# A block of RG-LRU, retention and gated MLP on one core: norm factors spread through DRAM, first loads on two queues, last scalings shared with GpSimd, one more buffer

## The chip, the cores and the metric

The kernel runs on one NeuronCore of a Trainium2 chip. The metric is the device time of one execution in microseconds, taken as the median over several runs. Profiles come from the hardware profiler, one execution each. In them PE is TensorE (PEld its weight loads), DVE VectorE, ACT ScalarE, POOL GpSimd and SP the sync engine, on whose queue nearly all transfers are issued.

## What is computed

One decoder block on x of shape (1, 2048, 1024) in float32. Cut to what matters:

```
u = rms_norm(x, norm1_gain);  proj = u @ w_in                  # 1024 -> 3072
x_lru, g_lru, q, k, v, g_ret = split(proj)
hl = rg_lru(causal_conv(x_lru))                                # a scan over the sequence
y_lru = rms_norm(hl * gelu(g_lru), lru_norm_gain)
o = head_group_norm(retention_chunkwise(rotary(q), rotary(k), v))
y_ret = o * silu(g_ret)
h = x + concat(y_lru, y_ret) @ w_out                           # 1024 -> 1024
u = rms_norm(h, norm2_gain)
a, b = split(causal_conv(u @ ffn_up_w))                        # 1024 -> 2 * 3072
h = h + (gelu(a) * b) @ ffn_down_w                             # 3072 -> 1024
out = rms_norm(h, final_norm_gain)
rms_norm(x, g) = x / sqrt(mean(x * x) + eps) * g               # one factor for each position
```

## The kernel before

Channels lie on the 128 partitions, positions on the free axis. The 2048 positions are two groups (g = 0, 1) of 1024, which the program calls HT. The stages follow one another on TensorE: A (input projection with the LRU and retention work) of g 0, A of g 1, B (output projection) of both, U (up projection, convolution, gate) of both, D (down projection in three parts c = 0, 1, 2) of both. A `Unit` multiplies two weight tiles of 128x1024 by the stage's input as seven block products of a Winograd scheme (p1 to p7, 12 matmuls each); a `PlainUnit` does eight ordinary quarter products of 12 matmuls. Each float32 operand is split into a high and a low part, both in the float32r form (`split`, `split_here`: ACT makes the high part, DVE the low one), and three matmuls stand for one product.

Work is held in SLOTS buffers of 128x1024 and eight PSUM banks. No instruction order is written out: generator processes ask for buffers, banks and operations, and `Flow` (lines 190 to 316) plays them against a cost for each operation (`Engine.cost_*`, `Op.kb` for a transfer) and gives each engine a fixed order, by readiness and a priority in ticks (one tick is one product). LEAD is how many ticks ahead weights may be asked for, RAW how many ticks ahead the split of an input block gets its priority. Every engine then runs its list in order, SP and ACT their transfers too.

A norm needs one factor for each position, and the positions lie along the free axis. `rstd` (line 985) sums the squares over partitions with one matmul for each 128 positions (tile `mst`), which puts the sums on partitions as [128, 8] (tile `ms`), scales them on DVE and raises them to -0.5 on POOL. `spread` (line 970) then makes the [128, 1024] tile `rb`, the same in every partition: eight matmuls of the broadcast factor column against the identity (tile `pb`, two groups of four), and two ACT copies from PSUM. It is called by `norm1` for both groups (line 1030), by the LRU norm of both groups (line 1123), by stage B's norm of both groups and stage D's of group 0 (`NormGroup`, line 1352), and for the last output three times on parts of 512, 256 and 256 positions (`FinalGroup.piece`, line 1400). DVE then multiplies the data by gain and `rb`.

At the start the raw x blocks of the first units are scaled by a gain column of the vector tile `vec` (`RawStage.bring`, line 548), and the first weight tile comes in two halves (`PlainUnit.first`, line 728).

Of the kernel before, what the change touches and what calls it, by code (L numbers as in the profile page):

```python
# [25 lines left out]
F32 = mybir.dt.float32  # L26
# [14 lines left out]
SLOTS = 54  # L41
# [3 lines left out]
BACKLOG = 10.0  # L45
RATE = 330.0
# [12 lines left out]
RAW = 3  # L59
LEAD = 10  # L60
# [42 lines left out]
class Engine:  # L103
# [55 lines left out]
    def cost_p(self, op, n, args, kw):  # L159
        return 1.0 if op != "dma_start" else 0.1  # L160
# [159 lines left out]
def hymba_block_kernel(ctx: ExitStack, tc: tile.TileContext, xh, xn, win, wout, wup, down, gates, vecs,  # L320
# [96 lines left out]
    vec = cp.tile([P, V_N], F32, name="vec")  # L417
    idt = cp.tile([P, P], F32, name="idt")
    sml = cp.tile([P, 2, NH], F32, name="sml")
    ones = cp.tile([P, P], F32, name="ones")  # L420
# [13 lines left out]
    def setup():  # L434
        yield v.memset(ones, 1.0)
        z = yield Slot("z")
        yield v.memset(z[:, 0:Q], 0.0)
        y = yield Bank("sm", "y0")
        for i in range(WARM):
            yield pe.matmul(y, ones, z[:, 0:Q], start=True, stop=True)  # L440
        free(z, y)
# [99 lines left out]
    class RawStage(Stage):  # L541
# [6 lines left out]
        def bring(self, name, i, need, start):  # L548
            k, n = int(name[0]) - 1, int(name[1]) - 1
            yield Until(start)  # L550
            r = yield (Slot("raw", F32R) if self.gain is None else Slot("raw"))
            if self.gain is None:
                yield from self.src[2 * k + i].get_half(r.bitcast(F32), n)
            else:
                for m in range(2):
                    yield dma(r[:, half(m)], self.src[2 * i + m].t[:, k, half(n)])
            yield need - 2
            if self.gain is None:
                self.blk[name, i] = yield from split_here(r, "b")
            else:  # L560
                hi = yield Slot("bh", F32R)
                lo = yield Slot("bl", F32R)
                for m in range(2):
                    yield a.activation(hi[:, half(m)], r[:, half(m)], AF.Copy, scale=col(self.gain + 4 * i + 2 * m + k))
                    yield v.scalar_tensor_tensor(out=lo[:, half(m)], in0=r[:, half(m)], scalar=col(self.gain + 4 * i + 2 * m + k),
                                                 in1=hi[:, half(m)].bitcast(F32), op0=ALU.mult, op1=ALU.subtract)
                self.blk[name, i] = (hi, lo)
                free(r)
            self.event(name, i).on = True
# [124 lines left out]
    class PlainUnit:  # L694
# [20 lines left out]
        def weights(self, t0):  # L715
# [21 lines left out]
            def part(i, need, k, r, hi, lo):  # L737
                yield dma(r[:, half(k)], self.wsrc[i][:, half(k)])
# [230 lines left out]

    def spread(rt, c0, c1, r):  # L970

        yield have["idt"]
        for b in range(c0, c1, Q):
# [7 lines left out]
            yield op  # L981
            yield a.copy(r[:, b - c0:b - c0 + w], pb[:, 0:w])
            free(pb)

    def rstd(acc, n, r, c0=0, c1=HT):

        nb = (c1 - c0) // P
        rt = sp.tile([P, NCH], F32, tag="ms", name="ms")[:, 0:nb]
        pm = yield Bank("sm", "mst")
        op = None  # L990
        for t in range(nb):
            o = pe.matmul(pm[:, t:t + 1], acc[:, c0 + t * P:c0 + (t + 1) * P], ones[:, 0:1], start=True, stop=True)
            op = op + o if op else o
# [4 lines left out]
        yield from spread(rt, c0, c1, r)  # L998
# [31 lines left out]
    def norm1(g, start, due):  # L1030

        ms = sp.tile([P, NCH], F32, tag="ms1", name="ms1")
        left = [NCH]

        def one(t):
# [6 lines left out]
            if left[0] == 0:  # L1042
# [3 lines left out]
                yield from spread(ms, 0, HT, r)  # L1046
# [346 lines left out]
    class FinalGroup(NormGroup):  # L1393
# [6 lines left out]
        def piece(self, m, t, c0, c1):  # L1400
# [127 lines left out]
    def vectors():  # L1528
        yield dma(vec, vecs)
# [111 lines left out]
```

## Time and profile before

| | us |
|---|---|
| median of 3 runs | 2193.12 (2189.13 to 2193.19) |
| the profiled execution's own time | 2191.24 |
| its span in the profile | 2189.1 |
| PE busy | 2159.5 |
| DVE, ACT, POOL busy | 1767.8, 1244.6, 44.4 |

The span is the time from the first to the last recorded instruction, 2.1 us less than the execution's own time. Busy times overlap between engines. A profile line names an operation by the tile that it writes and the tiles that it reads (`pb<-idt,ms`); a float32 matmul that is not float32r leaves two records.

### The profile page before, as it was taken

The numbers are of one execution on the slowest core, as the hardware profiler recorded it, in microseconds if no ns is written. First come the engines' busy times: TensorE is split into PE (matmuls) and PEld (weight loads), VectorE is DVE, ScalarE is ACT, GpSimd is POOL, SyncE is SP. The second block draws the span as 40 slices with busy tenths as digits, with TensorE's granted clock in tenths as the row PEclk, the third lists the DMA queues.
The fourth block names the chain that finished last, engine by engine and source line by source line (L and its number), as shares of the span: only waits on it lengthen the run. The fifth ranks groups of instructions, "written<-read, shape, count | busy, mean of one in ns | idle before, by whom it ended". The sixth has DMA issues, their size and how long they took to land.

```text
span 2189.1 us, 26790 instructions
## 1 busy us (share of the span) xinstructions
PE 2159.5 (99%) x9938; PEld 1781.6 (81%) x9938; DVE 1767.8 (81%) x2228; ACT 1244.6 (57%) x1795; POOL 44.4 (2%) x30
## 2 busy tenths in 40 slices
PE   9999999999999999999999999999999999999998
PEld 6878878888788888888888888888888788887887
DVE  6999888877773688889788997888878987788875
ACT  6774775566632166666666766666666544444441
POOL 0010000000000000000000000000000000000000
PEclk9999999999999999999999999999999999999999
DMA  8965464133674954444333532322335787589762
GB/s 324 368 211 194 134 215 157 61 117 98 205 258 149 381 193 145 163 158 150 102 97 139 212 113 90 116 94 101 113 121 180 267 308 261 219 295 348 267 252 77
DMA packets 140530, 407.83 MB, mean 186 GB/s; under 512 B 15728, under 2 KB 20208, under 8 KB 140400
## 3 DMA queue, kind: packets, MB, share of 16 engines
q1 hardware_dynamic: 139248, 405.08, 52.5%
q8 instruction: 78, 1.28, 0.2%
q10 hardware_dynamic: 1152, 1.05, 0.1%
q14 instruction: 52, 0.43, 0.1%
HBM read 272.63 MB, written 125.04 MB: 182 GB/s over the span
## 4 chain that ended last, share of the span: by engine, by line
PE 94%; DVE 2%; DMA 1%; ACT 1%; issue 1%; SPq 0%; POOL 0%; POOLq 0%; DVEq 0%
PE py L124 33%; PE px L124 22%; PE pe L124 22%; PE pq L124 12%; PE po L124 1%; PE pa L124 1%; PE pb L124 1%; PE sc L124 1%; PE pt L124 1%; PE pk L124 1%; DVE raw L124 0%; PE mst L124 0%; DVE res L124 0%; DMA h<-res 0%; DMA h<-h 0%
## 5 line engine op out<-in xcount | busy, mean ns | idle before, releaser
L124 DVE TENSOR_TENSOR wl<-s,wh 128x1024 fp32r<-128x1024 f32 x182 | 222.3, 1221 | 90.9 <-ACT wh L124 83.5
L124 PE MATMUL py<-bh,wh 128*128 128x512 f32 x728 | 285.8, 393 | 3.4 <-DVE res L124 2.4
L124 PE MATMUL px<-raw,wh 128*128 128x512 f32 x728 | 284.1, 390 | 4.8 <-DVE raw L124 4.8
L124 PE MATMUL px<-bh,wh 128*128 128x512 f32 x728 | 285.8, 393 | 0.1
L124 PE MATMUL pe<-bh,wl 128*128 128x512 f32 x728 | 283.5, 389 | 2.3 <-DVE wl L124 2.3
L124 ACT CAST wh<-s 128x1024 fp32r<-128x1024 f32 x182 | 190.8, 1048 | 166.6 <-DVE s L124 150.3
L124 PE MATMUL pe<-raw,wh 128*128 128x512 f32 x728 | 283.4, 389 | 1.5 <-DVE raw L124 1.5
L124 PE MATMUL pe<-bh,wh 128*128 128x512 f32 x728 | 284.6, 391 | 0.0
L124 PE MATMUL py<-bh,wl 128*128 128x512 f32 x728 | 284.1, 390 | 0.0
L124 PE MATMUL px<-bh,wl 128*128 128x512 f32 x728 | 284.0, 390 | 0.0
L124 PE MATMUL py<-raw,wh 128*128 128x512 f32 x728 | 283.8, 390 | 0.0
L124 DVE SCALAR_TENSOR_TENSOR c<-o,vec,c 128x1022 f32<-128x1022 f32 x192 | 244.4, 1279 | 6.2
L124 PE MATMUL py<-bh,wv 128*128 128x512 f32 x728 | 240.4, 391 | 2.2 <-ACT o L124 1.4
L124 ACT COPY o<-py 128x512 f32<-128x512 f32 x204 | 119.5, 586 | 188.7 <-PE py L124 188.0
L124 DVE TENSOR_TENSOR raw<-raw,bh 128x1024 fp32r<-128x1024 f32 x158 | 188.8, 1218 | 3.3 <-ACT bh L124 3.3
L124 ACT CAST bh<-raw 128x1024 fp32r<-128x1024 f32 x158 | 161.3, 1050 | 36.7 <-DMA raw<-g_T 12.4
L124 PE MATMUL pq<-bh,wh 128*128 128x512 f32 (+1 forms) x432 | 168.2, 389 | 1.1 <-ACT bh L124 1.1
L124 PE MATMUL pq<-bh,wl 128*128 128x512 f32 (+1 forms) x432 | 165.7, 383 | 0.0
L124 PEld LDWEIGHTS py<-bh,wh 128*128 128x128 f32 x728 | 137.1, 188 | 33.9 <-DVE res L124 2.9
L124 PEld LDWEIGHTS px<-bh,wh 128*128 128x128 f32 x728 | 136.8, 188 | 33.6 <-issue 2.8
L124 PEld LDWEIGHTS px<-raw,wh 128*128 128x128 f32 x728 | 137.0, 188 | 33.3 <-DVE raw L124 5.7
L124 PEld LDWEIGHTS py<-bh,wv 128*128 128x128 f32 x728 | 136.7, 188 | 33.3 <-ACT o L124 1.6
(137 smaller groups left out, 3848.5 us busy)
## 6 DMA issues: line engine op xcount, KB each, us to landing
wa<-in_dram SPq DMA_DIRECT2D x91, 512.0 KB, 3.8
wb<-in_dram SPq DMA_DIRECT2D x91, 512.0 KB, 4.7
h<-res SPq DMA_DIRECT2D x56, 512.0 KB, 3.6
g_T<-t SPq DMA_DIRECT2D x96, 256.0 KB, 2.3
raw<-g_T SPq DMA_DIRECT2D x48, 512.0 KB, 7.2
res<-h SPq DMA_DIRECT2D x48, 512.0 KB, 6.9
g<-c SPq DMA_DIRECT2D x76, 256.0 KB, 3.0
raw<-g SPq DMA_DIRECT2D x38, 512.0 KB, 8.1
```

The costliest lines, as they stand in the source:

```text
L124: return Op(self.name, lambda: fn(*args, **kw), us, writes, reads, func=func)
```

## The change

Six of the ten spreads (`norm1` of group 1, the LRU norm of both groups, stage B's of both and stage D's of group 0) go through DRAM: `spread_far` stores the factors from [128, 8] into a DRAM row of 1024 and reads the row back into all partitions with two broadcast transfers, all three on SP's queue. `norm1` of group 0 keeps the matmuls and the copies. The three spreads of the last output keep the matmuls, but DVE reads the PSUM tile `pb` directly. Of the last two parts (256 positions each) two of the eight tiles are scaled by their gain on ACT beforehand and by the factor on POOL, from an ACT copy of `pb`.

At the start the gains of the first norm get a tile of their own, loaded first on ACT's queue together with one half of the first weight tile; the big vector tile is loaded later, and the first high part is made on DVE. `ones` shrinks to one column, some small tiles have fewer buffers and the scratch for dynamic transfers is smaller; SLOTS goes from 54 to 55, LEAD from 10 to 12, RAW from 3 to 4. So `Flow` plans every engine's order anew.

```diff
-SLOTS = 54
+SLOTS = 55
+SMALL = 600
-RAW = 3
-LEAD = 10
+RAW = 4
+LEAD = 12
...
     def cost_p(self, op, n, args, kw):
-        return 1.0 if op != "dma_start" else 0.1
+        return 0.1 if op == "dma_start" else max(1.0, 0.3 + 2.2e-3 * n)
...
+    gain1 = cp.tile([P, KT], F32, name="gain1")
-    ones = cp.tile([P, P], F32, name="ones")
+    ones = cp.tile([P, 1], F32, name="ones")
...
-            yield pe.matmul(y, ones, z[:, 0:Q], start=True, stop=True)
+            yield pe.matmul(y, z[:, 0:P], z[:, 0:Q], start=True, stop=True)
...
             else:
+                if name == "11" and i == 0:
+                    yield -20
                 for m in range(2):
                     yield dma(r[:, half(m)], self.src[2 * i + m].t[:, k, half(n)])
...
-                    yield a.activation(hi[:, half(m)], r[:, half(m)], AF.Copy, scale=col(self.gain + 4 * i + 2 * m + k))
+                    gain = gain1[:, 4 * i + 2 * m + k:4 * i + 2 * m + k + 1]
+                    if name == "11" and i == m == 0:
+                        yield v.tensor_scalar(out=hi[:, half(m)], in0=r[:, half(m)], scalar1=gain, scalar2=None, op0=ALU.mult)
+                    else:
+                        yield a.activation(hi[:, half(m)], r[:, half(m)], AF.Copy, scale=gain)
...
-                yield dma(r[:, half(k)], self.wsrc[i][:, half(k)])
+                yield dma(r[:, half(k)], self.wsrc[i][:, half(k)], "sp" if k else "a")
...
+    def spread_far(rt, r):
+        row = dp.tile([NCH, P], F32, name="row", tag=f"row{len(rows)}")
+        rows.append(row)
+        there = row.rearrange("t p -> p t")
+        yield Op("sp", lambda: nc.sync.dma_start(there, rt), ISSUE, parts(row), parts(rt), kb=SMALL)
+        n = HT // 2
+        for h in range(2):
+            src = row[h * 4:h * 4 + 4].rearrange("(o t) p -> o (t p)", o=1).to_broadcast([P, n])
+            yield dma(r[:, half(h)], src)
...
             yield op
+            if r is None:
+                return pb
             yield a.copy(r[:, b - c0:b - c0 + w], pb[:, 0:w])
...
-        yield from spread(rt, c0, c1, r)
+        if r is None:
+            return (yield from spread(rt, c0, c1, r))
+        yield from spread_far(rt, r)
...
-                yield from spread(ms, 0, HT, r)
+                yield from spread_far(ms, r) if g else spread(ms, 0, HT, r)
...
-                r = yield Slot("rb")
-                r = r[:, 0:c1 - c0]
-                yield from rstd(self.ss.acc, D, r, c0, c1)
+                n_p = 2 if c0 else 0
+                ys = [t[:, c0:c1] for _, t in sorted(self.t.items())]
+                for k in range(n_p):
+                    yield a.activation(ys[k], ys[k], AF.Copy, scale=col(V_NF + k))
+                pb = yield from rstd(self.ss.acc, D, None, c0, c1)
                 yield 10 ** 5
-                for k in range(KT):
-                    y = self.t[k][:, c0:c1]
-                    yield v.scalar_tensor_tensor(out=y, in0=y, scalar=col(V_NF + k), in1=r, op0=ALU.mult, op1=ALU.mult)
+                if n_p:
+                    r = yield Slot("rb")
+                    yield a.copy(r[:, 0:c1 - c0], pb[:, 0:c1 - c0])
+                    fl.spawn(self.by_pool(ys[:n_p], r[:, 0:c1 - c0], c0, c1), 0)
+                for k, y in list(enumerate(ys))[n_p:]:
+                    yield v.scalar_tensor_tensor(out=y, in0=y, scalar=col(V_NF + k), in1=pb[:, 0:c1 - c0], op0=ALU.mult, op1=ALU.mult)
                     fl.spawn(self.out(k, y, c0, c1), 10 ** 6)
+        def by_pool(self, ys, r, c0, c1):
+            for k, y in enumerate(ys):
+                yield p.tensor_tensor(out=y, in0=y, in1=r, op=ALU.mult)
+                yield from self.out(k, y, c0, c1)
...
     def vectors():
+        yield dma(gain1, vecs[:, V_N1:V_N1 + KT], "a")
+        yield -1
         yield dma(vec, vecs)
...
-    nc = _bacc.Bacc("TRN2", target_bir_lowering=False, num_devices=1, dynamic_dma_scratch_size=1024)
+    nc = _bacc.Bacc("TRN2", target_bir_lowering=False, num_devices=1, dynamic_dma_scratch_size=256)
```

How the planned order moves stands at three places. The first is PE in stage B, at the norm of group 0 (`pq` is a quarter product's PSUM tile, `bh` and `raw` the high and low parts of an input block, `wh` and `wl` those of a weight). Before, from the end of the sums to the first group of the spread, the rows of the matmuls between standing four times:

```order
L124 MATMUL mst<-ones,sqacc 128x1 x8
L124 MATMUL pq<-bh,wh 128x512
L124 MATMUL pq<-raw,wh 128x512
L124 MATMUL pq<-bh,wl 128x512
...
L124 MATMUL pb<-idt,ms 128x128 x4
L124 MATMUL pq<-bh,wh 128x512
L124 MATMUL pq<-raw,wh 128x512
L124 MATMUL pq<-bh,wl 128x512
...
L124 MATMUL pb<-idt,ms 128x128 x4
```

```order
L125 MATMUL mst<-ones,sqacc 128x1 x8
L125 MATMUL pq<-bh,wh 128x512
L125 MATMUL pq<-raw,wh 128x512
L125 MATMUL pq<-bh,wl 128x512
L125 MATMUL pq<-bh,wh 128x512
L125 MATMUL pq<-raw,wh 128x512
L125 MATMUL pq<-bh,wl 128x512
```

In the changed order no `pb` follows; the next row that is not a product is the sum of the next norm.

The second is SP in stage A of group 1, at the fifth of the 91 `wa` loads of the program (`wa` and `wb` are the two weight tiles of a Unit, `x_11` to `x_22` DRAM blocks of the normed input, `sw` the rotary's swapped halves). Before:

```order
L356 DMA x_22_0_265<-x 128x512
L356 DMA x<-in_dram 128x1024
L356 DMA sw<-o_1364 64x1024 x2
L356 DMA x<-in_dram 128x1024
L356 DMA wa<-in_dram 128x1024
L356 DMA wb<-in_dram 128x1024
L356 DMA x_11_1_254<-x 128x512
```

Now:

```order
L357 DMA x_22_0_266<-x 128x512
L357 DMA wa<-in_dram 128x1024
L357 DMA x<-in_dram 128x1024
L357 DMA wb<-in_dram 128x1024
L357 DMA sw<-o_1360 64x1024 x2
L357 DMA x<-in_dram 128x1024
L357 DMA x_11_1_255<-x 128x512
```

The weight load has moved ahead of three issues that it stood behind.

The third is SP in stage D of group 1, where stage D's norm of group 0 falls (`h_3` holds the sums to be normed, `res<-h_0` and `h_1_2<-res` belong to the running stage). Before:

```order
L356 DMA raw<-g_1_11_1_209 128x1024
L356 DMA res<-h_0_1_109 128x1024
L356 DMA h_1_2_114<-res 128x1024
L356 DMA res<-h_0_3_111 128x1024
L356 DMA h<-h_3_0_104 128x1024
L356 DMA h<-h_3_1_105 128x1024
```

Now:

```order
L357 DMA raw<-g_1_11_1_210 128x1024
L983 DMA row<-ms 128x8x1
L357 DMA res<-h_0_1_110 128x1024
L357 DMA res<-h_0_3_112 128x1024
L357 DMA rb<-row 128x512 x2
L357 DMA h_1_2_115<-res 128x1024
L357 DMA h<-h_3_0_105 128x1024
L357 DMA h<-h_3_1_106 128x1024
```

The row's store, which waits for POOL, now stands ahead of two `res` loads, and its two reads, which wait for the store to land, ahead of the `h` loads.

## Rows read from the trace of the kernel before

**Rows 1.** The page: the span, and busy time of the engines.

```profile
span 2189.1 us, 26790 instructions
PE 2159.5 (99%) x9938; PEld 1781.6 (81%) x9938; DVE 1767.8 (81%) x2228; ACT 1244.6 (57%) x1795; POOL 44.4 (2%) x30
```

**Rows 2.** Timeline of PE: four of the eleven gaps from 100 to 2150.

```profile
112.35 0.50 PE L124 MATMUL px<-raw,wh 128*128 128x512 f32 x1 [1.34 <-DVE raw L124]
...
181.66 0.50 PE L124 MATMUL pe<-bh,wl 128*128 128x512 f32 x1 [2.26 <-DVE wl L124]
...
315.33 0.79 PE L124 MATMUL px<-raw,wh 128*128 128x512 f32 x1 [3.50 <-DVE raw L124]
...
2146.82 0.50 PE L124 MATMUL py<-bh,wv 128*128 128x512 f32 x1 [0.78 <-DVE res L124]
```

**Rows 3.** Groups of PE instructions, forms apart: busy, mean ns, idle before.

```profile
L124 PE MATMUL pb<-idt,ms 128*128 128x128 f32 x128 | 18.1, 284 | 1.6 <-POOL ms L124 1.6
```

**Rows 4.** Chain of waits, 823 to 838: start, us, what.

```profile
826.43 2.89 PE pe L124 x12
...
829.32 1.16 PE pb L124 x8
830.48 2.77 PE pe L124 x12
833.25 0.89 PE pb L124 x8
```

**Rows 5.** Chain of waits, whole span: one of its longest pieces.

```profile
710.48 76.20 PE pq L124 x336
```

**Rows 6.** Stretches: length, busy of PE, PEld, DVE, ACT, POOL, granted clock, DMA.

```profile
73.00:146.00 73.00, 71.37 (x363) 58.31 (x362) 68.53 (x101) 59.96 (x81) 6.36 (x3) 1.00 0.73 279
306.00:322.00 16.00, 12.50 (x46) 9.72 (x44) 15.16 (x15) 13.51 (x17) 0.00 (x0) 0.79 0.50 169
657.00:730.00 73.00, 73.00 (x338) 60.67 (x337) 34.24 (x39) 15.63 (x16) 2.55 (x1) 1.00 0.57 206
1970.00:1985.00 15.00, 14.88 (x66) 12.01 (x65) 10.10 (x11) 3.21 (x4) 0.00 (x0) 1.00 0.95 341
```

**Rows 7.** Stretches at the start, same columns.

```profile
0.00:13.00 13.00, 9.38 (x19) 4.03 (x19) 6.71 (x14) 7.71 (x11) 0.20 (x4) 1.00 0.85 295
13.00:17.00 4.00, 3.74 (x9) 2.68 (x10) 3.96 (x8) 3.97 (x5) 0.00 (x0) 0.57 1.05 391
```

**Rows 8.** Chain of waits at the start.

```profile
1.18 0.42 SPq L356
...
5.57 6.67 DMA raw<-in_dram
...
13.26 23.51 PE pq L124 x95
```

**Rows 9.** Timeline of the last 10 us.

```profile
2180.06 0.87 POOL L124 TENSOR_TENSOR ms<-ms,cst 128x2 f32<-128x2 f32 x1 [5.75 <-DVE ms L124]
...
2182.24 0.37 ACT L124 COPY rb<-pb 128x256 f32<-128x256 f32 x1 [3.67 <-PE pb L124]
...
2182.65 3.25 DVE L124 SCALAR_TENSOR_TENSOR res<-res,vec,rb 128x256 f32<-128x256 f32 x8 [0.29 <-ACT rb L124]
```

**Rows 10.** DMA view: queue, packets, MB, share; then issues, KB each, us to landing.

```profile
q1 hardware_dynamic: 139248, 405.08, 52.5%
...
z<-z SPq DMA_DIRECT2D x8, 512.0 KB, 5.4
...
state<-kT SPq DMA_DIRECT2D x4, 64.0 KB, 2.1
```

**Rows 11.** Chain of waits, 170 to 184.

```profile
172.91 7.42 DMA wa<-in_dram
```

**Rows 12.** Timeline of SP, stage A of group 1.

```profile
169.43 0.46 SPq L356 DMA_DIRECT2D x<-in_dram  x1
```

**Rows 13.** Timeline of DVE in stage B.

```profile
715.94 1.28 DVE L124 SCALAR_TENSOR_TENSOR h<-h,vec,rb 128x1024 f32<-128x1024 f32 x1 [5.63 <-DMA h<-h]
```

More of the change, by code (lines that the diff above doesn't have):

```diff
@@ L563, in bring @@
                 for m in range(2):
-                    yield a.activation(hi[:, half(m)], r[:, half(m)], AF.Copy, scale=col(self.gain + 4 * i + 2 * m + k))
-                    yield v.scalar_tensor_tensor(out=lo[:, half(m)], in0=r[:, half(m)], scalar=col(self.gain + 4 * i + 2 * m + k),
+                    gain = gain1[:, 4 * i + 2 * m + k:4 * i + 2 * m + k + 1]
[3 more added lines that the diff above has]
+                        yield a.activation(hi[:, half(m)], r[:, half(m)], AF.Copy, scale=gain)
+                    yield v.scalar_tensor_tensor(out=lo[:, half(m)], in0=r[:, half(m)], scalar=gain,
                                                  in1=hi[:, half(m)].bitcast(F32), op0=ALU.mult, op1=ALU.subtract)
@@ L968, in add @@
             self.left -= 1
+    def spread_far(rt, r):
[7 more added lines that the diff above has]
+            yield dma(r[:, half(h)], src)
+    rows = []
     def spread(rt, c0, c1, r):
@@ L987, in rstd @@
         nb = (c1 - c0) // P
-        rt = sp.tile([P, NCH], F32, tag="ms", name="ms")[:, 0:nb]
+        rt = sp.tile([P, NCH], F32, tag="ms", name="ms", bufs=2)[:, 0:nb]
         pm = yield Bank("sm", "mst")
@@ L991, in rstd @@
         for t in range(nb):
-            o = pe.matmul(pm[:, t:t + 1], acc[:, c0 + t * P:c0 + (t + 1) * P], ones[:, 0:1], start=True, stop=True)
+            o = pe.matmul(pm[:, t:t + 1], acc[:, c0 + t * P:c0 + (t + 1) * P], ones, start=True, stop=True)
             op = op + o if op else o
@@ L1030, in norm1 @@
     def norm1(g, start, due):
-        ms = sp.tile([P, NCH], F32, tag="ms1", name="ms1")
+        ms = sp.tile([P, NCH], F32, tag="ms1", name="ms1", bufs=1)
         left = [NCH]
@@ L1408, in piece @@
             if self.count % 2 == 0:
-                r = yield Slot("rb")
-                r = r[:, 0:c1 - c0]
-                yield from rstd(self.ss.acc, D, r, c0, c1)
-                yield 10 ** 5
-                for k in range(KT):
-                    y = self.t[k][:, c0:c1]
-                    yield v.scalar_tensor_tensor(out=y, in0=y, scalar=col(V_NF + k), in1=r, op0=ALU.mult, op1=ALU.mult)
-                    fl.spawn(self.out(k, y, c0, c1), 10 ** 6)
+                n_p = 2 if c0 else 0
[3 more added lines that the diff above has]
+                pb = yield from rstd(self.ss.acc, D, None, c0, c1)
+                yield 10 ** 5
+                if n_p:
[4 more added lines that the diff above has]
+                    yield v.scalar_tensor_tensor(out=y, in0=y, scalar=col(V_NF + k), in1=pb[:, 0:c1 - c0], op0=ALU.mult, op1=ALU.mult)
+                    fl.spawn(self.out(k, y, c0, c1), 10 ** 6)
+                free(pb)
+        def by_pool(self, ys, r, c0, c1):
+            for k, y in enumerate(ys):
+                yield p.tensor_tensor(out=y, in0=y, in1=r, op=ALU.mult)
+                yield from self.out(k, y, c0, c1)
         def out(self, k, y, c0, c1):
```

## The prediction

> **What bounds the kernel.** I read the page first. PE is busy for 2159.5 of 2189.1 us, DVE for 1767.8 [rows 1], so only work taken off PE, or idle time of PE that disappears, can show in the end. Where the idle 29.6 us lie comes from the timeline of PE: eleven gaps between 100 and 2150 sum to 15.9, the longest 3.50 [rows 2]; the other 13.7 are at the two ends. The long gaps are waits for a low part that DVE had not yet made (`raw`, `wl`), so data and DVE's order set them. The stretches tell how much room DVE has: in stage A it works 68.5 of 73 us, and 15.2 of the 16 around the longest gap; in stage B 34.2 of 73 [rows 6]. In those 16 us the granted clock is 0.79 instead of 1.00: after the 3.50 us gap PE ran for a while at the lower of its two levels, 1.2 GHz, so a long gap costs more than its length.
>
> The sum is made against the profiled execution's own time, 2191.24 us, which is its span and 2.1 around it; the median shown, 2193.12, is 1.9 above that. A measurement of this kernel can tell about 0.2% from no change: 2188.7 to 2197.5 counts as the same.
>
> **Spreads leave PE.** Six spreads of eight matmuls go; the first order piece shows PE's list without them. The cost of one is read from the chain in stage U [rows 4]. From 826.43 to 830.48 lie one product and half a spread, 4.05 us; from 830.48 to 833.25 + 0.89 the same again, 3.66. A product of 12 matmuls without neighbours takes 76.20 / 336 x 12 = 2.72 [rows 5]. Of the first piece, 0.17 is the pipeline filling after the sums (2.89 instead of 2.72), which stays. So a spread costs 4.05 + 3.66 - 2 x 2.72 - 0.17 = 2.10, and six 12.6. The group view bounds it from above: 18.1 us for 128 records, of which 96 go, 13.6 [rows 3]; the chain's shorter piece from below, 12 x 0.89 = 10.7. I take **-12.4**, the chain's value rounded a little towards the lower end. The twelve ACT copies go too; ACT works 1244.6 us of the span [rows 1], so that is worth nothing.
>
> **What takes their place.** A store of 1024 factors, each to a place of its own, and two broadcast reads of 256 KB, all on SP. No row shows such a store. From below it costs what a small store over 128 partitions costs, 2.1 us to landing [rows 10]. From above: queue 1's packets kept 16 engines busy for 52.5% of 2189.1 us, which is 132 ns for each of 139248; 1024 words as a packet each are 64 for each engine, 8.5 us. The reads cost from 2.1 to 5.4 (`z<-z` has as many bytes as both) [rows 10]. I take 5 and 4, near the middle: the packets are many but tiny, and the reads are nearest to `z<-z`. So `rb` is there 9 us after POOL (4 to 14), where matmuls and copies needed 4.8 (829.32 to 834.14 [rows 4]) and one more copy, some 5.4: 3.6 us later than before.
>
> Behind it wait, on SP, what is planned after the reads (the `h` or `z` loads that the scaling needs too, `h_1_2`, later `wa` and `wb`), and on DVE everything behind the first scaling by `rb`: in stages B and D the additions that free PE's banks. Cover is there. None of the six norms feeds the next product, weights may be asked for 12 ticks of 2.72 us ahead, and in stage B a DVE wait of 5.63 us for `h` in just this place left PE without a gap [rows 13]. In stages A and D DVE is dense and the 3.6 us can come through. I take **+2.0** for all six, between 0 (all hidden, as in stage B) and 10.8 (3.6 at each of three dense places), nearer to the former because the one row that shows such a wait shows it hidden.
>
> A rule speaks against this part. The page DMA: Bandwidth & Descriptors of the Trainium skill (section Specifications) says that for pieces below 512 B the engine reads, changes and writes back. No run here shows pieces so small; by the rule the store would stand at its upper bound or past it, which is the first rival below.
>
> **The gaps, planned anew.** The whole order is a new plan, so any gap may move. One has a visible cause: at 181.66 PE waited 2.26 for a low part [rows 2] whose weight tile was issued at 172.91 and took 7.42 to land [rows 11]. In the new order (second piece) this load stands ahead of an `x` load, two `sw` and another `x`, which kept SP from 169.43 on [rows 12]; 3.5 us earlier is more than the gap. I take **-2.0**. The 3.50 gap I leave: both orders have 21 block splits ahead of DVE's scan there, so the same split waits behind the scan. RAW = 4 asks for splits a tick earlier but does not change that count. The other gaps stay, with bounds of -6 and +6.
>
> **The start.** A `raw` load issued at 5.57 lands 6.67 later, PE runs through from 13.26 [rows 8], and from 13 to 17 the granted clock is 0.57, the lower level, after the pauses before it [rows 7]. In the new order 2.6 MB instead of 3.3 are loaded up to the end of the first eight `raw` loads, because `vec` and a whole weight tile have moved behind. At the 295 GB/s of the first 13 us [rows 7] 0.65 MB are 2.2 us. But that weight tile then comes later, and PE needs it after 24 matmuls, about when it has landed and been split. So the start lies between a gain of 3.5 (2.2 and most of the 1.7 us that 4 us at 0.57 lose) and a loss of 1.0 (a wait for that tile); I take **-1.5**.
>
> Issuing on two queues is by itself worth little: SP needs 0.42 us for one issue [rows 8], and 256 KB at 295 GB/s take 0.89. The same page of the Trainium skill (section Issuing engines are not separate DMA queues) says that several issuers save only the time of issuing; by it alone the start would gain 0.4, one issue, and the trace agrees in that moving is slower than issuing.
>
> **The end.** After the last factor come an ACT copy of 0.37 and eight DVE scalings in 3.25 [rows 9]. DVE now starts without the copy and does six: 0.4 + 2 x 0.41 = 1.2 less. POOL's two start after the copy, at 2182.62. If one takes what POOL's shortest row here does, 0.87 [rows 9], they end at 2184.4, before DVE's six (2184.7). At POOL's mean, 44.4 us for 30 [rows 1], they end at 2185.6, 0.9 after them. I take **-1.0**, bounds -1.2 and +1.0. Warm-up, `ones`, scratch and the smaller buffers move no work of a bounded engine: nothing.
>
> **Sum.** 2191.24 - 12.4 + 2.0 - 2.0 - 1.5 - 1.0 = **2176.3 us**.
>
> **The rivals.**
> 1. *The store holds up the queue* (slower). With the store at 8.5 and the reads at 5.4, `rb` is 8.5 us late. SP stands at the read, DVE at the first scaling, PE at the next low part or addition. At the three places with the least cover (group 1's first norm and group 0's LRU norm, both in dense stage A, and stage D, where the DMA engines are 95% busy [rows 6]) that is 25.5 in place of the 2.0: 2199.8. It decides for slower from 7.7 us at each. For it: the third order piece has the store ahead of loads that the running product needs. Against it: the lead of 12 ticks, and DMA engines half idle on average [rows 10]. Chance 0.05.
> 2. *The new plan brings gaps of its own.* If the 15.9 us of gaps double, the time is 2192.2. For it: every list changes, and the plan does not know what lands late. Against it: two more ticks of lead and one more buffer. Chance 0.10.
> 3. *Stage A is DVE's.* Where DVE works 68.5 of 73 us [rows 6], what PE no longer does turns into waiting for DVE. Two of the six spreads lie there: 4.2 come back, 2180.5. For it: the gaps there are waits for DVE [rows 2]. Against it: PE was busy for 71.4 of the same 73. Chance 0.15.
> 4. *The plan clears more.* If the two gaps behind block splits in stage A go (1.34 and 3.50 [rows 2]) and with them a spell at the low clock, 1.7 as at the start, 6.5 more are won: 2169.8. For it: RAW = 4. Against it: the count of splits. Chance 0.15.
>
> **How the numbers follow.** My forecast has the remaining 0.55. The range runs from 2165 (rival 4 with the start and the spreads at their better bounds) to 2189 (the forecast with the row's cost, the end and the spreads at their worse bounds); outside lie rivals 1 and 2, 0.15. Faster by over 0.2%: the forecast and rivals 3 and 4, 0.85; the same: rival 2, 0.10; slower: rival 1, 0.05.
>
> **What would show it.** `pb` has 32 records and some 4.5 us instead of 128 and 18.1; in stages B and U products follow one another every 2.72 us through the norms; `row` lands within 2 to 8.5 us; the 2.26 gap is gone; the last scalings end 1 us sooner after the last `pb`. I am wrong if PE's gaps between 100 and 2150 sum to more than 25 us, or if a gap stands where DVE waits for `rb`.

## The result and the profile after

The changed kernel takes **2202.91 us** (median of 6 runs, 2198.11 to 2208.01) where the kernel before took 2193.15 in the same series: a ratio of 1.0046, 95% interval 1.0029 to 1.0064. It is slower by over 0.2%. The forecast was 2176.3, and "faster".

First the page, of the changed kernel (a helper's line moved, so L125 here is L124 before, and SP's DMA issues are L357):

```profile
span 2198.7 us, 26605 instructions
PE 2153.8 (98%) x9842; PEld 1773.6 (81%) x9842; DVE 1761.3 (80%) x2225; ACT 1242.3 (57%) x1785; POOL 41.3 (2%) x34
```

PE is busy for 5.7 us less than before [rows 1], and the span is 9.6 longer: about 15 us more of it are idle on PE. The spreads did go, as the group of `pb` shows (32 records instead of 128, 4.6 us instead of 18.1 [rows 3]):

```profile
L125 PE MATMUL pb<-idt,ms 128*128 128x128 f32 x32 | 4.6, 281 | 1.9 <-POOL ms L125 1.9
```

The DMA view (queue, packets, MB, share; then issues, KB each, median us to landing) has what took their place:

```profile
q1 hardware_dynamic: 147072, 407.99, 53.2%
...
z<-z SPq DMA_DIRECT2D x8, 512.0 KB, 7.5
rb<-row SPq DMA_DIRECT2D x12, 256.0 KB, 6.5
row<-ms SPq DMA_DIRECT2D x6, 4.0 KB, 9.1
```

A store of 4 KB takes 9.1 us to land. It is 1024 words, each with a place of its own. Queue 1 has 7824 packets more than before, and `z<-z` lands in 7.5 instead of 5.4 [rows 10]. The waits of SP's queue (whole span: us in total, times, longest) show how long it stood still for the landing:

```profile
SPq L983 <- POOL ms L125: 55.9, 6, 28.6
...
SPq L357 <- DMA row<-ms: 47.8, 6, 8.6
...
SPq L357 <- POOL res L125: 7.5, 2, 4.7
```

That is 8.0 us for each of six norms in which SP, which issues nearly every transfer, stands still before the first read of `row`. It also stands still before each store until POOL has the factors (the first line); `after_packed` below has that wait too (56.4 us) without the loss. What the wait for the landing costs shows in stage D, in the chain of waits from 1945 to 1982:

```profile
1955.30 9.26 DMA row<-ms
...
1964.62 0.32 SPq L357
...
1966.82 8.16 DMA h<-h
...
1975.10 1.21 DVE h L125
1976.31 1.22 DVE wl L125
1977.52 0.61 DVE res L125
...
1978.17 4.21 PE px L125 x9
```

The `h` that is scaled first is issued only when the row has landed, takes 8.16 itself, and behind the scaling stand on DVE a low part and the addition that frees PE's bank. The timelines of DVE and PE have the two waits, one passed on to the other:

```profile
1975.10 1.28 DVE L125 SCALAR_TENSOR_TENSOR h<-h,vec,rb 128x1024 f32<-128x1024 f32 x1 [6.91 <-DMA h<-h]
```

```profile
859.95 0.79 PE L125 MATMUL py<-bh,wh 128*128 128x512 f32 x1 [3.99 <-ACT o L125]
...
1978.17 0.80 PE L125 MATMUL px<-bh,wh 128*128 128x512 f32 x1 [5.68 <-DVE res L125]
```

PE's gaps between 100 and 2150 sum to 26.9 us instead of 15.9. The two above each stand behind a store; the kernel before has no gap at the first place and one of 2.44 us in stage D. Two shorter ones stand behind earlier stores:

```profile
131.12 0.66 PE L125 MATMUL pa<-xc,ea 64*128 64x512 f32 x1 [2.23 <-DMA ea<-in_dram]
...
632.92 0.49 PE L125 MATMUL po<-st,o 128*128 128x128 f32 x2 [1.45 <-DVE st L125]
```

At 131 PE waits for a load (`ea`) that SP issued behind the reads of the first row; at 633 it waits for DVE, which had stood 8.52 us for a `z` issued behind the reads of the third. After each of the two long gaps, PE runs at the lower of its two levels for a while, as after the 3.50 us gap before: stretches of the changed kernel (length, busy of PE, PEld, DVE, ACT, POOL, granted clock, DMA):

```profile
1972.00:1988.00 16.00, 10.32 (x37) 8.03 (x36) 10.97 (x11) 1.62 (x2) 0.00 (x0) 0.79 0.96 346
856.00:864.00 8.00, 4.05 (x12) 3.27 (x13) 7.66 (x9) 5.64 (x10) 0.00 (x0) 0.79 0.54 164
```

The end lost too. From the last `pb` (2186.70) to the end of the span are 12.0 us, before 8.1. SP's list has the outputs of GpSimd's two tiles ahead of four finished ones of 256 KB, and waits 7.5 us for `POOL res` (above) while the DMA engines are nearly idle (the second number from the right):

```profile
2184.00:2188.00 4.00, 1.29 (x8) 1.04 (x8) 3.53 (x10) 1.77 (x5) 1.60 (x3) 0.91 0.19 66
2188.00:2192.00 4.00, 0.00 (x0) 0.00 (x0) 2.29 (x6) 0.00 (x0) 1.98 (x3) 0.50 0.82 291
```

The start gained 2.1 us: the first `pb` begins at 34.51 instead of 36.61.

### The profile page after: what moved, and what is told of

Its sections match the earlier page's. It is cut to its first block, busy times and chain, and to the rows that moved or that the text cites. A ratio compares the mean times of both kernels' runs of the same rounds, so it can differ in the third digit from the quotient of the medians.

```text
span 2198.7 us, 26605 instructions
## 1 busy us (share of the span) xinstructions
PE 2153.8 (98%) x9842; PEld 1773.6 (81%) x9842; DVE 1761.3 (80%) x2225; ACT 1242.3 (57%) x1785; POOL 41.3 (2%) x34
## 4 chain that ended last, share of the span: by engine, by line
issue 57%; PE 33%; DMA 5%; DVE 3%; ACT 1%; POOL 0%; SPq 0%; DVEq 0%; ACTq 0%; POOLq 0%
PE py L125 10%; PE pq L125 7%; PE px L125 6%; PE pe L125 6%; PE po L125 1%; DMA row<-ms 1%; PE pa L125 1%; PE sc L125 1%; PE pk L125 1%; PE pt L125 1%; DMA raw<-in_dram 1%; DMA xt<-in_dram 0%; DMA x<-in_dram 0%; DVE xc L125 0%; DVE res L125 0%
## 5 line engine op out<-in xcount | busy, mean ns | idle before, releaser
L125 DVE TENSOR_TENSOR wl<-s,wh 128x1024 fp32r<-128x1024 f32 x182 | 222.2, 1221 | 99.3 <-ACT wh L125 91.3
L125 PE MATMUL px<-bh,wh 128*128 128x512 f32 x728 | 287.0, 394 | 6.4 <-DVE res L125 5.7
L125 PE MATMUL py<-bh,wh 128*128 128x512 f32 x728 | 286.3, 393 | 4.3 <-ACT o L125 4.0
L125 PE MATMUL px<-raw,wh 128*128 128x512 f32 x728 | 284.8, 391 | 3.5 <-DVE raw L125 3.5
L125 PE MATMUL pe<-bh,wh 128*128 128x512 f32 x728 | 284.9, 391 | 1.7 <-DVE o L125 1.6
L125 PE MATMUL py<-bh,wl 128*128 128x512 f32 x728 | 284.2, 390 | 1.1 <-DVE wl L125 1.1
L125 PE MATMUL pe<-raw,wh 128*128 128x512 f32 x728 | 283.6, 390 | 1.6 <-DVE raw L125 1.6
L125 PE MATMUL px<-bh,wl 128*128 128x512 f32 x728 | 284.7, 391 | 0.0
L125 PE MATMUL py<-raw,wh 128*128 128x512 f32 x728 | 284.0, 390 | 0.0
L125 PE MATMUL pe<-bh,wl 128*128 128x512 f32 x728 | 283.5, 389 | 0.0
L125 ACT CAST wh<-s 128x1024 fp32r<-128x1024 f32 x182 | 191.0, 1050 | 158.5 <-DVE s L125 135.5
L125 DVE SCALAR_TENSOR_TENSOR c<-o,vec,c 128x1022 f32<-128x1022 f32 x192 | 244.1, 1279 | 8.6 <-ACT c L125 4.6
L125 PE MATMUL py<-bh,wv 128*128 128x512 f32 x728 | 242.4, 394 | 1.7 <-ACT o L125 0.9
L125 ACT COPY o<-py 128x512 f32<-128x512 f32 x204 | 119.8, 587 | 174.9 <-PE py L125 174.0
L125 DVE TENSOR_TENSOR raw<-raw,bh 128x1024 fp32r<-128x1024 f32 x158 | 189.8, 1218 | 18.0 <-ACT bh L125 17.9
L125 ACT CAST bh<-raw 128x1024 fp32r<-128x1024 f32 x158 | 162.3, 1049 | 48.2 <-DMA raw<-g_T 11.0
L125 PEld LDWEIGHTS px<-bh,wh 128*128 128x128 f32 x728 | 137.4, 189 | 39.8 <-DVE res L125 6.1
L125 PE MATMUL pq<-bh,wh 128*128 128x512 f32 (+1 forms) x432 | 167.7, 388 | 0.7 <-ACT wh L125 0.7
L125 PEld LDWEIGHTS py<-bh,wh 128*128 128x128 f32 x728 | 137.2, 189 | 35.2 <-ACT o L125 5.2
L125 PE MATMUL pq<-bh,wl 128*128 128x512 f32 (+1 forms) x432 | 165.2, 383 | 0.2 <-DVE wl L125 0.2
L125 PEld LDWEIGHTS py<-bh,wv 128*128 128x128 f32 x728 | 138.2, 190 | 33.7 <-DVE res L125 1.2
L125 PEld LDWEIGHTS px<-raw,wh 128*128 128x128 f32 x728 | 137.6, 189 | 31.7 <-DVE raw L125 3.8
```

The source lines that it names most:

```text
L125: return Op(self.name, lambda: fn(*args, **kw), us, writes, reads, func=func)
```

## The experiments

Each number stands beside the kernel before, run on the same chip; its medians there ran from 2190.6 to 2192.9. So a difference between kernels of two series carries some 2 us of doubt, and their ratios to the kernel before are the safer measure. Theory R: the rows come late and hold up SP and DVE. Theory P: the new order, or the other parts of the change, cost the time. Theory T: the end is held by GpSimd's two tiles.

### One part undone, or one alone

`row_off`: all of the change but the rows.

```
-        yield from spread_far(rt, r)
+        yield from spread(rt, c0, c1, r)
...
-                yield from spread_far(ms, r) if g else spread(ms, 0, HT, r)
+                yield from spread(ms, 0, HT, r)
```

> The changed kernel with all six DRAM rows undone (matmuls and ACT copies again); start, last scalings, 55 buffers, LEAD 12 and RAW 4 kept. Theory R (the store's 9.1 us to landing, planned as 3.5, keeps SP and then DVE waiting): the gaps at 856 and at 1972 go or fall below 2.5 us, PE's 12.6 us of spreads come back, and the time is 2190 to 2196. Theory P (the new plan with 55 buffers, LEAD 12 and RAW 4 makes the gaps by itself): the gaps stay, and with the spreads back the time is 2212 to 2218.

Measured 2190.29, ratio 0.9994 (0.9985 to 1.0004). The rows are 12.6 us of harm (11.4 by the ratios), net of the spreads that they save; the gaps at 856 and 1973 are gone. P as it was put falls. But the order is planned anew here too, so this run does not part the rows from the order that they brought; `after_packed` below does.

`row_only`: the kernel before, with the six rows and nothing else.

> The kernel before with only the six DRAM rows put in; 54 buffers, LEAD 10, RAW 3, the start and the end as before. Theory R: the stores land in 9 us here too and new gaps of 3 to 6 us stand after them, so that at most half of the 12.6 us are won: 2184 to 2196. Theory P: without the new constants the rows win what was forecast, 2178 to 2182.

Measured 2214.85, ratio 1.0101 (1.0085 to 1.0116), worse than either theory said. In PE's timeline the gaps are of the same kind and longer:

```profile
762.59 0.79 PE L125 MATMUL pq<-bh,wl 128*128 128x512 f32 x1 [8.82 <-DVE wl L125]
...
1999.30 0.77 PE L125 MATMUL px<-bh,wh 128*128 128x512 f32 x1 [9.41 <-DVE res L125]
```

The rows cost 22 us here and 12.6 in the changed kernel. Whether its longer lead, its 55th buffer or its other order takes off the difference was not tried.

`pool_off`: no last scalings on GpSimd.

```
-                n_p = 2 if c0 else 0
+                n_p = 0
```

> The changed kernel with all eight last scalings of each part on DVE from PSUM, none on POOL. Theory T (SP's output queue stands behind POOL's two tiles of the second part, 7.5 us, while four ready outputs of 256 KB wait behind them): from the last product to the end of the span it takes 3 to 4.5 us less than in the changed kernel, and the whole 3 to 4.5 us less. Rival (the end is bound by the bytes to write): within 1 us of the changed kernel, or slower by the 0.8 us of two more DVE scalings.

Measured 2200.05, ratio 1.0034 (1.0022 to 1.0047). The 2.9 us are just under T's 3, and the intervals of the two kernels overlap. The end itself is clear: from the last `pb` to the end are 7.9 us instead of 12.0 although DVE has GpSimd's four tiles to scale as well, and SP no longer waits for GpSimd. T holds for the end.

`plan_9us`: the changed kernel, the plan told that a store takes 9 us (1.7 + 2450 / 330) instead of 3.5. Nothing else differs.

```
-SMALL = 600
+SMALL = 2450
```

> The changed kernel with the store's cost in the plan raised from 3.5 to 9.1 us (SMALL 600 to 2450), what the profile shows; nothing else. Theory R with the plan as cause: the order no longer puts DVE's scalings ahead of data that is late, the 5.67 us gap falls below 2.5, and the time is 2192 to 2197. Rival (the harm is SP standing still, which no order repairs): within 3 us of the changed kernel.

Measured 2191.39, ratio 0.9996 (0.9988 to 1.0005): a plan that knows of the store loses nothing against the kernel before, but wins nothing either. The time is just under the expected range; the gap in stage D is not as expected, it still has 4.48 us.

### Together, and the queue by itself

> The plan told that a store takes 9 us (2191.4) and GpSimd given none of the last scalings (2200.1 alone) in one kernel. If the two harms stand apart, their gains add: 2191.4 - 2.9 = 2188.5, range 2185 to 2191, below the kernel before (2192.7), and the last sum of squares to the end is back from 26.4 to about 22.5 us. If the end only hides what the rows delay, the time stays at 2191 to 2193.

`plan_pool` takes 2186.11, ratio 0.9974 (0.9965 to 0.9982): the gains add, with -5.3 for the end (-4.8 by the ratios) instead of -2.9.

> No rows and no GpSimd scalings: what is left of the change is the start, the 55th buffer, the earlier blocks and the other lead. Alone without rows it was 2190.3. If the end costs the same 3 to 4 us here, 2186 to 2188; if the start's 2.1 us is all that is left as a gain, 2190.6. Neither theory has the kernel above 2192.

`both_off` takes 2185.97, ratio 0.9976 (0.9967 to 0.9986). With neither rows nor GpSimd, what is left of the change (the start, the buffer, the lead, DVE reading `pb` at the end) is a gain of 6.9, or 5.3 by the ratio.

`store_idle` has the spreads on PE again and also issues the six stores, which nobody reads.

> The spreads are on TensorE again as in the kernel before, and the six stores of 1024 words are still issued, with no reads of them and nobody who waits: what the store costs the queue and the transfers beside it, alone. Theory Q (the words hold up what is queued behind them in the rings): transfers issued right behind a store land up to 6 us late, the gap near 1972 is there again, and the time is 3 to 8 us above the kernel without rows (2190.3), 2193 to 2198. Theory H (only SyncE's standing still behind a store that it must see land, and the late factors, cost): no difference over 1.5 us, 2189 to 2192.

Measured 2201.38, ratio 1.0044 (1.0030 to 1.0058): 11 us above `row_off`, more than Q said, with no wait for a row to land left in it. That speaks for Q, but the order had changed as well; `idle_packed` below keeps it. `row_rows` stores the factors as rows: PE transposes, ACT copies, and 8 pieces of 512 bytes go out. Cut to what matters:

```
-        there = row.rearrange("t p -> p t")
-        yield Op("sp", lambda: nc.sync.dma_start(there, rt), ...)
...
+        yield pe.matmul(pb[0:NCH, 0:P], rt, idt, start=True, stop=True)
+        eight = r[0:NCH, 0:P]
+        yield a.copy(eight, pb[0:NCH, 0:P])
...
+        yield Op("sp", lambda: nc.sync.dma_start(row, eight), ...)
```

> The six stores carry 8 pieces of 512 bytes instead of 1024 words of 4: TensorE transposes the 128x8 factors (one product) and ScalarE copies the 8x128 result, a little under 1 us of the two in a line; the cost given to the store in the plan stays 1.8 us + 1.7 us. Theory W (the words are what makes the store long): row lands within 2 to 4 us of its issue instead of 9.1, SyncE's wait on it falls from 6.7 to 8.6 us to below 3, the gap at the last stage (5.67 us) and the clock losses behind it go, and the time is 2180 to 2192. Theory R' (a DRAM row is slow whatever its pieces, because a write and a read after it take their round trips): row still lands 6 us or more after its issue, and the time stays within 5 us of the changed kernel, 2198 to 2206.

Measured 2189.08, ratio 0.9988 (0.9979 to 0.9997). W holds: in stage D the reads of `row` are issued 3.6 us after the store instead of 9.3, and PE's gap there is 2.15 instead of 5.68.

### The pieces alone, every order kept

`after_packed` and `idle_packed`: one line, in the changed kernel and in `store_idle`. In `after_packed` the factors then stand in another order in the row than the columns, so it tells of time alone. Every engine's order is that of the kernel that it is compared with.

```
-        there = row.rearrange("t p -> p t")
+        there = row.rearrange("t p -> (t p)").rearrange("(p t) -> p t", t=NCH)
```

> The changed kernel with every instruction and every order on every engine as it is; only the store's addresses differ: the 128x8 factors go out as they lie, 128 pieces of 32 bytes in place of 1024 of 4 (the factors then stand in another order in the row, so the columns get the wrong ones; no time hangs on the values). Theory W (the number of pieces is the cost): row lands in 2 to 4 us instead of 9.1, SyncE's standing behind it falls from 6.7 to 8.6 us to under 3, the gaps after the stores at 856 and 1973 go, and the time falls from 2202.9 to 2186 to 2195. Theory O (the order that the plan chose is bad by itself, the pieces only a part): the time stays above 2197.

Measured 2181.43, ratio 0.9951 (0.9940 to 0.9963): **21.5 us** less than the changed kernel (20.8 by the ratios) and below the expected range. Its DMA view and SP's waits:

```profile
rb<-row SPq DMA_DIRECT2D x12, 256.0 KB, 4.4
row<-ms SPq DMA_DIRECT2D x6, 4.0 KB, 1.8
```

```profile
SPq L357 <- DMA row<-ms: 6.2, 5, 2.0
```

The same 4 KB from the same tile land in 1.8 us as 128 pieces, and in 9.1 as 1024. SP waits 6.2 us for it in all instead of 47.8, and no gap of over 0.5 us follows a store. By where the sums of squares begin, the two kernels part as follows (us, changed minus packed, one profile each): LRU norm of group 0 +0.1, of group 1 +0.4, stage B +3.9, group 1's +4.4, stage D +10.5, the last norm +17.8, the end +17.4. The first store does cost some 3 us at 131, but most of that is made up at 252, where PE waits 1.62 us for DVE and in the packed kernel 3.37, so stage A loses nothing on balance. The 3.5 up to stage B's norm are the gaps at 633 and 651, behind the store of group 1's LRU norm; the 6.1 before stage D are the gap at 856 and the clock behind it, the 7.3 behind it those at 1973.

> The kernel of the unread stores (2201.4), again with every order as it is and only the pieces changed, 128 of 32 bytes for 1024 of 4. Theory Q (the 1024 pieces hold up what is queued behind them): h<-h falls from a median of 12.2 us to landing to about 6, and the time falls to that of the kernel without rows, 2188 to 2193. Theory O (the reordering that six more transfers bring into the plan is what cost those 11 us): it stays at 2198 to 2202.

Measured 2192.67, ratio 1.0006 (0.9997 to 1.0015), 8.7 less than `store_idle`. The DMA views, first 1024 pieces, then 128:

```profile
h<-h SPq DMA_DIRECT2D x24, 512.0 KB, 12.2
...
row<-ms SPq DMA_DIRECT2D x6, 4.0 KB, 10.6
```

```profile
h<-h SPq DMA_DIRECT2D x24, 512.0 KB, 6.1
...
row<-ms SPq DMA_DIRECT2D x6, 4.0 KB, 1.6
```

So the pieces hold up the transfers behind them: `h<-h` takes twice as long where nobody waits for the store at all. That is Q, shown with every order kept. Whether they wait in SP's queue or for the DMA engines is not shown: between 100 and 2150 us every transfer is on that queue.

### Versions with the factors in the right order

> The whole change mended in two places: rows stored as 8 pieces of 512 bytes (2189.1 alone) and no GpSimd scalings at the end (-2.9 where it was tried). If the two add: 2186, range 2184 to 2188, the last sum of squares to the end back at 22 to 23 us. If the rows are worth their 2.1 us of TensorE each, it should beat the kernel without rows and without GpSimd scalings (2186.0) by some us, to 2176 to 2182; if the rows are worth nothing even when short, it stands within 2 us of it.

`rows_best` takes 2184.17, ratio 0.9967 (0.9955 to 0.9978): the two gains add, but it beats `both_off` by less than 2 us, so with PE's transposition and an order of its own it shows little of the spreads' worth.

`best` packs the factors in the right order by giving each of the sums' products every eighth column as its weights. Cut to that:

```
-            o = pe.matmul(pm[:, t:t + 1], acc[:, c0 + t * P:c0 + (t + 1) * P], ones, ...)
+            cols = slice(c0 + t * P, c0 + (t + 1) * P) if r is None else slice(t, HT, NCH)
+            o = pe.matmul(pm[:, t:t + 1], acc[:, cols], ones, ...)
```

> The packed store made right, and no GpSimd scalings: chunk t of a sum of squares takes the columns t, t+8, t+16, ... so that the 128x8 factors lie in the order of the row and go out as 128 pieces of 32 bytes; every engine's order is that of the kernel of pool_off (2200.1). If the gains of the packed store (-21.5 us in the changed kernel) and of the end (-2.9) add: 2178.5, range 2175 to 2182, below the kernel before (about 2192) and below the one without rows and without GpSimd scalings (2186.0). If reading every eighth column as weights, or rows of x eight apart, costs what the packing gains, it stands at 2184 or above; if the end's 2.9 us was only there because the rows ran late, at 2181 to 2182.

Measured 2191.62, ratio 1.0004 (0.9995 to 1.0013): the middle case, far above its lower end. Chain of waits from 600 to 618:

```profile
606.02 3.74 PE mst L125 x16
609.77 4.26 PE pq L125 x12
```

The 16 products of a sum take 3.74 us instead of 1.84, and the product behind them 4.26 instead of 2.72 [rows 5]: in the stretches after it the granted clock is 0.86 and 0.71 (1.00 in both in `packed_pool`, with plain columns).

```profile
604.00:608.00 4.00, 4.00 (x19) 3.52 (x17) 3.42 (x4) 0.91 (x1) 0.00 (x0) 1.00 0.00 0
608.00:612.00 4.00, 4.00 (x16) 3.59 (x17) 2.20 (x4) 1.06 (x1) 1.63 (x1) 0.86 0.17 65
612.00:616.00 4.00, 4.00 (x16) 3.15 (x16) 3.11 (x3) 0.59 (x1) 0.00 (x0) 0.71 0.39 111
```

> Every order of the kernel of strided columns (2191.6), with plain columns (the factors then stand in another order in the row). If the strided weight loads are its cost (3.74 to 3.94 us for 16 products instead of 1.84, and a granted clock of 0.50 to 0.86 in the stretches behind them): 2177 to 2181, the gains of the packed store and of the end added. If the end or the chip's state is the cost: 2188 to 2192.

`packed_pool`, with the order of `best`, plain columns and plain rows of x (and so the factors in another order than the columns again), takes **2175.21**, ratio 0.9928 (0.9915 to 0.9942). The reordering cost 16 us; `sq_read` below, with the same strided rows of x, stands 3 us above `packed_pool`, so it was the weights. `packed_pool` and `pool_off` are a third pair that differs in the line of the store alone, with every engine's order the same: 24.8 us (23 by the ratios).

`best2` lets PE sum straight into rows of [8, 128], with GpSimd's power on those.

> The sums over partitions are taken by eight products with weights of 8 columns (ones in column t, else zeros) that add up in one bank: the 8x128 factors come out as rows, are scaled and raised to the power there, and go out as 8 pieces of 512 bytes; only the first norm's second half keeps rows of x eight apart and 128 pieces of 32 bytes. No product and no copy more than in the changed kernel. No GpSimd scalings. The order is planned anew. If the store's pieces and the strided weights were all that stood in the way: 2175 to 2182, the fastest of all. If GpSimd's power over 128 columns a partition instead of 8 (0.7 to 0.9 us before) takes some us and the factors come late again: 2184 to 2190, with gaps near 856 and 1973.

Measured 2263.02, ratio 1.0330 (1.0314 to 1.0347), far outside both. POOL's groups say why:

```profile
L125 POOL TENSOR_TENSOR rb<-rb,cst 8x128 f32<-8x128 f32 x5 | 111.7, 22341 | 1362.8 <-DVE rb L125 1362.8
...
L125 POOL TENSOR_TENSOR ms<-ms,cst 128x8 f32<-128x8 f32 x2 | 4.1, 2044 | 108.1 <-DVE ms L125 108.1
```

The same 1024 powers take 22.3 us on 8 partitions and 2.0 on 128: the factors come 20 us late. (The 0.7 to 0.9 us of the expectation are those of the last norm's 128x2.)

`sq_read` and `sq_write` reorder in ACT's squares, by strided reads or strided writes, with the order of `packed_pool`. Of `sq_read`, cut to what matters:

```
+            if self.far:
+                out = out.rearrange("q (t p) -> q t p", t=NCH)
+                src = src.rearrange("q (p t) -> q t p", t=NCH)
+            return a.activation(out, src, AF.Square)
```

> Every engine's order is that of packed_pool (2175.2); only ScalarE's 32 squares of 128x1024 on these paths read every eighth column, so that the sums of squares stand chunk by chunk in the order in which the packed row needs them (and the second half's rows of x are eight apart). If ScalarE reads strided columns at its speed (1.06 us each): 2174 to 2178, and the sums' products stay at 1.84 us. If each square takes twice as long, the 32 us fall on an engine that is 57% busy and only the last square of each of five sums is waited for: 2178 to 2186.

> As sq_read, with the reads in order and every eighth column written. At ScalarE's speed: 2174 to 2178. If a strided write costs what a strided weight load did (1.7 times): 2177 to 2186.

`sq_read` takes **2178.30**, ratio 0.9933 (0.9919 to 0.9946), `sq_write` 2179.79, 0.9936 (0.9924 to 0.9949). ACT's groups, before the reordering (`packed_pool`) and with it (`sq_read`):

```profile
L125 ACT ACTIVATE sqt<-res 128x1024 f32<-128x1024 f32 x26 | 27.6, 1060 | 93.3 <-DVE res L125 76.5 <-DVE rs L125 9.1 <-issue 7.6
```

```profile
L125 ACT ACTIVATE sqt<-res 128x1024 f32<-128x1024 f32 x26 | 51.4, 1978 | 84.4 <-DVE res L125 65.7 <-DVE rs L125 9.4 <-issue 9.3
```

A strided square takes 2.20 us by reads and 2.08 by writes instead of 1.06 (five of the 26 are not strided), some 37 us in all over 32 of them, on an engine with room for it. Of that 1 us by the ratios, or 3 by the medians, reaches the end in `sq_read`, and the intervals overlap with that of `packed_pool`. Both versions have the factors in the right order and beat both kernels: `sq_read` is 24.6 us below the changed one and 13.9 below the one before.

## Why the prediction was wrong

**The step that failed is "What takes their place": +2.0.** Undoing the pieces alone gives back 21.5 us (20.8 by the ratios). Three things in that step:

- *The store's size.* I took 5 us, between 2.1 and 8.5, "near the middle: the packets are many but tiny". It is 9.1, past the upper bound, which came from the mean time of a packet. Tiny packets cost what a packet costs: 9.1 us over 64 for each engine are 142 ns, where the row gave 132 [rows 10]; against the store of 128 pieces, 56 more for each engine cost 7.3 us, 130 ns each (an estimate, with the pieces spread evenly over 16 engines). The value had to be taken at that end.
- *What it holds up.* I counted who waits for `rb`. I did not count that a transfer behind the store in the queue waits for its pieces. `store_idle` against `idle_packed` shows 8.7 us of that with nobody reading a row.
- *The cover.* I leaned on stage B's wait of 5.63 that cost PE nothing [rows 13], as "the one row that shows such a wait", and on the 12-tick lead. The trace of the kernel before has another one, in stage D's norm, which PE did feel. DVE stands there for `h` and then for a store, and PE behind it for an addition, in its second-longest gap (I had put the long gaps down to low parts):

```profile
1982.86 1.28 DVE L124 SCALAR_TENSOR_TENSOR h<-h,vec,rb 128x1024 f32<-128x1024 f32 x1 [3.88 <-DMA h<-h]
1987.02 1.23 DVE L124 TENSOR_TENSOR wl<-wa,wh 128x1024 fp32r<-128x1024 f32 x1 [2.88 <-DMA h<-res]
...
1990.70 0.50 PE L124 MATMUL py<-bh,wh 128*128 128x512 f32 x1 [2.44 <-DVE res L124]
```

  And stage B's cover was worth 5.63 us of one wait; here SP issues nothing for 8 us, so the next loads are late together, and the order behind them was planned for 3.5 us (`plan_9us`: 11.5 us of the loss, 11.0 by the ratios, go when the plan knows).

Rival 1 was the right mechanism: SP at the read, DVE at the first scaling, PE at the next addition, and its 2199.8 is near 2202.9. That nearness is partly luck: it has 25.5 where the pieces cost 21.5, and nothing of the end's 6.2. Its chance of 0.05 was the misjudgement, and its places were half right. Stage D lost 7.3 (it said 8.5); group 1's first norm lost some 3 that came back later in the stage, group 0's LRU norm nothing; and instead group 1's LRU norm (3.5) and stage B's second norm (6.1) lost.

The rule that I weighed against this part, pieces below 512 B, pointed the right way. By that page of the Trainium skill (DMA: Bandwidth & Descriptors, Specifications) the store would be at or past its bound, and the trace agrees with 9.1. But 32-byte pieces are below 512 B too and land in 1.8 us. The line that fits both is in the same page of the Trainium skill, section Rules for kernel authors: a transfer whose last dimension is strided or not contiguous becomes one descriptor per element, so it should be rearranged. The trace agrees: with 128 pieces instead of 1024, queue 1 has 5376 packets less, six times 896.

**The spreads: -12.4, with 2.0 for a cheap row: -10.4 in all.** `packed_pool` against `both_off`, which differ in the rows and the order that follows from them, is -10.8. This term was right once the store was what the step had supposed. Rival 3 (stage A is DVE's), which gives 4.2 of it back, is thereby unlikely. The trace of stage A does not settle it: at group 1's LRU norm, where two spreads have gone, `packed_pool` is 6.5 us ahead of `both_off`, but `after_packed`, in the same order up to there, only 2.4.

**Gaps -2.0 and start -1.5.** `both_off` has both and gains 6.9 (ratio 0.9976: 5.3). The start's share is 2.1, right; the gap at 181.66 shrank to 1.12 in the changed kernel, not to nothing; the 3.50 gap stayed, as said. PE's gaps in `both_off` sum to 14.4 instead of 15.9, and from the last sum of squares to the end it takes 9.2 instead of 10.0. These and the start make 4.4; what is left of its gain was not taken apart.

**The end: -1.0.** The scalings do end sooner after the last `pb`, 3.6 us instead of 4.9, as worked out. But I stopped at the last scaling: two outputs were planned onto SP's queue ahead of finished ones, and the transfers that end the program waited. Giving GpSimd nothing gains 2.9 to 6.2 in five pairs (2.9 in the changed kernel, 4.3 without rows, 5.3 with the other plan, 4.9 with short rows, 6.2 with packed ones), by the ratios 2.6 to 5.0. In the traces the end itself, from the last sum of squares on, is 4.2 to 4.6 us shorter in each pair, so most of that spread is probably doubt between series. GpSimd's tiles with their outputs behind the others were not tried.

Put in a row, with the steps measured: 2192.9 - 6.9 (what `both_off` leaves) - 10.8 (spreads against packed rows) + 6.2 (GpSimd at the end) + 21.5 (1024 pieces) = 2202.9. The row closes because each step is the difference of two of the kernels; by the ratios the steps are -5.3, -10.5, +5.0 and +20.8. Without the last two it is the 2175.2 of `packed_pool`, 1.1 below the forecast, and that is partly luck: the kernel before stands 1.7 higher than in the sum, the first step gains 3.4 more than the forecast for gaps and start, and the end's -1.0 is not in it. (The range's lower end comes to 2166.6 from the bounds named for it, not 2165; nothing hangs on that.)

Of the announced signs, `pb` and the end of the last scalings came as said. The row's landing came later than its range, the 2.26 gap shrank without going, and the gap at 856, behind stage B's second norm, breaks the run of products. Of the signs of being wrong, the sum of the gaps came (26.9, over 25), and the gap behind DVE in another form: `rb` had landed at 1972.4, and DVE waited until 1975 for the `h` issued behind its reads.

## What to carry to other kernels

Count the pieces of a small transfer, not its bytes, and ask what stands behind it in its queue as well as who waits for it: 4 KB in 1024 pieces cost 21.5 us more over six stores than the same 4 KB in 128 pieces, whose six stores unread cost no more than 2.4 (`idle_packed` against `row_off`, within the noise). When a layout has to be turned round, put the stride on an engine with slack (ACT's squares: 1 to 3 us, within the noise) and not on PE's weights (16 us), nor on few partitions (20 us each time). And follow the end past the last computation, to the order in which the last transfers are issued.

## What the runs showed of the hardware

- A strided weight load costs PE nearly twice: 334 instead of 192 ns with every eighth column of 4 bytes, and in the 4 us stretches behind 16 of them the granted clock fell to 0.50 to 0.86 (0.50 from 832 to 836 in `best`). ACT pays the same for strided squares, 2.20 us by reads and 2.08 by writes instead of 1.06. A page of the Trainium skill (SBUF — State Buffer, Door 1: The DMA port swizzle) says that accesses within one 16-byte line run at full speed and each new line costs, so that for fp32 a stride is free up to four values. Steps of 32 bytes agree with it in direction, on both engines.
- GpSimd's power goes by columns and hardly by partitions: 22.3 us for 8x128, 2.0 for 128x8, 0.75 for 128x2 in the same run (`best2`).
- One profile differs from the next by some us even where every order is the same: `after_packed` and `packed_pool`, alike up to the last part and run on two chips, reach stage D's norm at 1940.92 and 1936.90. Positions in single profiles carry that much doubt; the medians above carry the argument.
